# Layer 1's first 32-slot expert placed between the two fixed experts in the order of use

## The chip, the cores and the metric

The kernel runs on one core of a Trainium2 chip. The metric is the device time of one execution in microseconds (us), the median of three executions. Matrix products run on TensorE (PE), evictions and elementwise work on VectorE (DVE) and ScalarE (ACT), index work on GpSimd (POOL), and the transfers of weights from HBM to SBUF are issued by SyncE (SP).

## The reference

The model is a trunk of two layers over 256 latent tokens and 256 context tokens, D = 1024. Each layer mixes tokens and then applies a mixture of experts: a shared router picks two of 16 experts for each token, and an expert is a gated feed-forward with 512 hidden columns. In the last layer only the 256 latent tokens are used, so 512 assignments are spread over 16 experts.

```python
u = jax.nn.silu(xb @ w1[e]) * (xb @ w3[e])      # 1024 -> 512, twice
return (u @ w2[e]) * wt[:, None]                # 512 -> 1024, weighted
...
return jnp.zeros_like(h).at[buf_tok].add(y)     # summed back into the tokens
```

After layer 1's experts a residual sum and a final RMSNorm give the output. Everything is float32.

## The kernel before

The change concerns the experts of layer 1, the last part of the program, in `moe(1)`, whose matmuls run from about 1195 us to 1437 us of the trace.

**Experts and slots.** The experts have fixed numbers of token slots. Experts 0 and 1 are "fixed" (`s0`, `s1`): 96 slots each, handled as 64 + 32. The other 14 are ranked on the chip by how many tokens chose them and go by their rank, 0 to 13: ranks 0 and 1 have 96 slots, 2 to 5 have 64, 6 to 13 have 32 (`DCAP`). Which expert's weights a rank needs is known only after the router, so their loads read an expert number into a register first (L1631), and the address is computed from it. The weights of s0 and s1 have known addresses.

**Steps.** An expert is 12 chunks of weights of 128x1024 (512 KB): 8 "up" chunks (w1 and w3 for 128 rows of D) and 4 "down" chunks (w2). `steps_of(l)` turns the order of use into steps: the 8 up steps of an expert, then the 4 down steps of the expert before it in the order. One step is one chunk: `up()` (L1487) multiplies it with the gathered tokens `xs` and sums in PSUM; `down()` (L1550) multiplies it with the transposed hidden values `uf`. A chunk of a 64 + 32 expert takes two matmuls of 64 rows x 512 columns and four of 32 rows x 256 columns; a chunk of a 32-slot expert takes the four alone. The small matmuls use 64-column or 32-column parts of the array, placed by `tile_position`.

**What follows an up block.** With the last up chunk ACT takes silu (L1497) and DVE the product (L1498); both read the PSUM tile `mm`, of which layer 1 has two. Then `turn()` transposes u on PE (L1518), four steps later as a rule. The down results go to `ys`, and once a unit of 128 slots is complete, `combine` scales it and PE adds it into the tokens' accumulators (L1449).

**Gathered tokens.** `batch()` gathers the tokens of several experts at once by one-hot matmuls (L1386) and turns the one-hot table for the combine (L1372). The third batch holds ranks 6 to 13. A batch is started up to `LEAD` = 14 steps ahead of the first step that needs it, one piece a step.

**Weights and buffers.** `fetch()` issues the load of each step's chunk on SP in the order of the steps (L1634), as far ahead as a buffer is free. There are 25 buffers: 16 `eraw`, in use since the token mixing, and 9 `eraw2`. `expert_raw()` takes them by a running number i: of each 25, the first 16 from the one pool and the next 9 from the other. The 24 chunks of s0 and s1 are loaded before the router ends: 16 into `eraw`, 6 into `eraw2` (L1024), two into a spare part of another tile (`xT`). Three `eraw2` are left for the first loads of a ranked expert; every later load waits until PE has used the chunk whose buffer it takes. 168 such loads follow (14 experts of 12 chunks). SP never has more than eight of them outstanding, each with a semaphore of its own.

**Order.** The order of use of layer 1 is a table, `ORDER1` (L80). PE's instructions stand in the order of the steps, with transposes, gathers and combines put between them.

Of the kernel before, what the change touches and what calls it, by code (L numbers as in the profile page):

```python
# [76 lines left out]
NRAW = (13, 16)  # L77
LENT = (tuple(("y", i) for i in (16, 17, 18)), ())
ORDER0 = ("s0", "s1", 13, 0, 12, 1, 11, 2, 9, 3, 4, 8, 5, 6, 7, 10)
ORDER1 = ("s0", "s1", 13, 12, 11, 10, 0, 9, 1, 8, 2, 3, 7, 4, 5, 6)  # L80
ORDER = (ORDER0, ORDER1)
LEAD = 14
OVERFLOW0 = (6, 11)
# [1849 lines left out]
```

## Time and profile before

| | |
|---|---|
| time before, median of 3 (lowest to highest) | 1469.04 us (1467.43 to 1472.51) |
| the profiled execution's own time | 1461.18 us |
| its span in the trace | 1459.1 us |
| PE busy over the span | 1336.4 us (92%) |
| first matmul of an expert of layer 1 to last | about 1195.8 to 1437.4 us |
| HBM read over the span | 344.39 MB, 246 GB/s |

The trace is of one execution; its own time is what the terms of a sum are added to. Shares over the span mix the token mixing, where PE is the limit, with the experts, where the weights must be streamed, so the stretch from 1195 us on is read by itself.

### The profile page before, as it was taken

How to read it: one execution, taken by the hardware profiler on the slowest of the kernel's cores; microseconds unless marked ns; L12 is line 12 of the kernel's file. 1: busy time of each engine (PE TensorE's matmuls, PEld its weight loads, DVE VectorE, ACT ScalarE, POOL GpSimd, SP SyncE). 2: the span in 40 equal slices, each digit the busy share in tenths (PEclk: the TensorE clock that was granted, in tenths of full speed). 3: DMA queues.
4: the chain of work that ended last, by engine and by line, in shares of the span. 5: the costliest groups of instructions: out<-in, count | busy, mean ns of one | idle time of the engine just before them, and what ended most of it. 6: DMA issues, size and time to landing. Idle time of an engine off the chain costs nothing. (4 is left out here: it accounts for less than half of the span.)

```text
span 1459.1 us, 22788 instructions
## 1 busy us (share of the span) xinstructions
PE 1336.4 (92%) x8584; PEld 919.1 (63%) x8584; DVE 782.9 (54%) x1488; ACT 525.6 (36%) x834; POOL 134.5 (9%) x163
## 2 busy tenths in 40 slices
PE   4899999999999998999899669999999979999875
PEld 2677677777788675655556257778799843534323
DVE  2896775464545365555566248877655572322113
ACT  2523543432223223445555234255354431212102
POOL 0000000131211021012000030001022000000000
PEclk9999999999999999999999879999999979999996
DMA  9777222233362279999999585753259547999993
GB/s 353 256 279 278 66 91 90 88 130 130 130 210 100 81 275 328 358 410 410 410 410 385 185 332 184 277 178 117 91 182 355 192 156 251 369 408 409 408 409 129
DMA packets 99682, 361.14 MB, mean 247 GB/s; under 512 B 11504, under 2 KB 13680, under 8 KB 99312
## 3 DMA queue, kind: packets, MB, share of 16 engines
q1 hardware_dynamic: 91376, 331.97, 61.2%
q0 software_dynamic: 8192, 27.66, 5.0%
q8 instruction: 69, 1.13, 0.3%
q14 instruction: 45, 0.37, 0.1%
HBM read 344.39 MB, written 15.20 MB: 246 GB/s over the span
## 5 line engine op out<-in xcount | busy, mean ns | idle before, releaser
L527 PE MATMUL mm<-hH,whi 128*128 128x512 f32 (+1 forms) x928 | 323.8, 350 | 4.3 <-ACT k L947 2.2
L528 PE MATMUL mm<-hL,whi 128*128 128x512 f32 (+1 forms) x928 | 318.6, 344 | 1.5 <-DVE hL L409 1.5
L529 PE MATMUL mm<-hH,wlo 128*128 128x512 f32 (+1 forms) x928 | 318.6, 344 | 0.1
L216 DVE TENSOR_TENSOR wlo<-raw,whi 128x1280 fp32r<-128x1280 f32 (+1 forms) x124 | 186.2, 1503 | 66.4 <-ACT whi L215 65.5
L215 ACT ACTIVATE whi<-raw 128x1280 fp32r<-128x1280 f32 (+1 forms) x124 | 144.9, 1169 | 167.1 <-PE mm L528 99.3
L527 PEld LDWEIGHTS mm<-hH,whi 128*128 128x128 f32 x928 | 177.1, 191 | 41.1 <-issue 16.7
L529 PEld LDWEIGHTS mm<-hH,wlo 128*128 128x128 f32 x928 | 177.0, 191 | 27.8 <-issue 7.9
L528 PEld LDWEIGHTS mm<-hL,whi 128*128 128x128 f32 x928 | 177.3, 191 | 22.0 <-issue 2.3
L1487 PE MATMUL mm<-eraw,xs 128*32 128x256 f32 (+1 forms) x1376 | 164.7, 455 | 13.5 <-DMA eraw<-wexp_d 6.8
L216 DVE TENSOR_TENSOR wlo<-eraw,whi 128x1024 fp32r<-128x1024 f32 x96 | 115.6, 1223 | 29.9 <-ACT whi L215 24.8
L1487 PEld LDWEIGHTS mm<-eraw,xs 128*32 128x32 f32 (+1 forms) x1376 | 50.3, 119 | 108.5 <-issue 70.3
L215 ACT ACTIVATE whi<-eraw 128x1024 fp32r<-128x1024 f32 x96 | 99.4, 1056 | 32.1 <-PE mm L1480 20.2
L947 ACT ACTIVATE k<-mm,hbg 128x512 f32<-128x512 f32 (+1 forms) x64 | 37.2, 581 | 161.5 <-PE mm L529 161.5
L1498 DVE TENSOR_TENSOR u<-u,mm 64x256 f32<-64x256 f32 (+1 forms) x27 | 14.0, 531 | 136.5 <-ACT u L1497 136.3
L953 POOL TENSOR_TENSOR acc<-acc,k 128x512 f32<-128x512 f32 (+1 forms) x48 | 50.6, 1054 | 320.8 <-DVE k L952 320.8
L952 DVE SCALAR_TENSOR_TENSOR k<-k,mm 128x512 f32<-128x512 f32 (+1 forms) x48 | 26.6, 554 | 93.8 <-PE mm L529 93.8
L1550 PE MATMUL mm<-eraw,uf 128*32 128x256 f32 (+1 forms) x560 | 65.3, 442 | 3.6 <-DVE u L1498 1.7
L1497 ACT ACTIVATE u<-mm 64x256 f32<-64x256 f32 (+1 forms) x27 | 12.5, 465 | 154.0 <-PE mm L1487 154.0
L1479 PE MATMUL mm<-wlo,xh 128*128 128x512 f32 x128 | 51.7, 404 | 1.7 <-DVE wlo L216 1.6
L1480 PE MATMUL mm<-whi,xl 128*128 128x512 f32 x128 | 50.2, 392 | 0.0
L1478 PE MATMUL mm<-whi,xh 128*128 128x512 f32 x128 | 46.2, 412 | 3.3 <-ACT whi L215 3.3
L818 ACT ACTIVATE k<-aux,sm 128x512 f32<-128x512 f32 (+1 forms) x48 | 29.2, 613 | 47.8 <-DVE sm L816 43.9
(388 smaller groups left out, 1964.4 us busy)
## 6 DMA issues: line engine op xcount, KB each, us to landing
eraw<-wexp_d SPq DMA_DIRECT2D x379, 512.0 KB, 10.1
raw<-wgb_d SPq DMA_DIRECT2D x64, 640.0 KB, 3.9
mb<-wmod_d SPq DMA_DIRECT2D x48, 512.0 KB, 5.4
raw<-win_d SPq DMA_DIRECT2D x40, 512.0 KB, 6.5
mraw<-wmod_d SPq DMA_DIRECT2D x16, 512.0 KB, 5.2
raw<-wo_d SPq DMA_DIRECT2D x16, 512.0 KB, 3.5
eraw<-wmod_d SPq DMA_DIRECT2D x12, 512.0 KB, 5.4
ybuf<-k POOLq DMA_DIRECT2D x9, 512.0 KB, 3.3
```

Of the source, the lines that this page charges most:

```text
L215: S.activation(hi, src, AF.Copy)
L216: V.tensor_sub(lo, src, hi.bitcast(F32))
L527: PE.matmul(ps[:, :T_], lhsT=hi[:, ws], rhs=xh(xs), start=(i == 0), stop=False)
L528: PE.matmul(ps[:, :T_], lhsT=hi[:, ws], rhs=xl(xs), start=False, stop=False)
L529: PE.matmul(ps[:, :T_], lhsT=lo[:, ws], rhs=xh(xs), start=False, stop=(i == N - 1))
L947: S.activation(t, ps[:, :T], AF.Tanh, scale=0.5, bias=hbg[:, br * 8 + m:br * 8 + m + 1])
L953: ga = G.tensor_add(acc[:, m], acc[:, m], pr)
L1478: PE.matmul(ps, lhsT=xh[:, k], rhs=hi[:, o:o + 512], start=(k == 0), stop=False)
L1479: PE.matmul(ps, lhsT=xh[:, k], rhs=lo[:, o:o + 512], start=False, stop=False)
L1480: PE.matmul(ps, lhsT=xl[:, k], rhs=hi[:, o:o + 512], start=False, stop=(k == KT - 1))
L1487: PE.matmul(ps[n * g:n * g + n, :w], lhsT=xin[x, s0][0][:, k], rhs=r[:, g * w:(g + 1) * w], start=(k == 0), stop=(k == KT - 1), tile_posit ...
L1550: PE.matmul(e["pys", s0][n * g:n * g + n, :w], lhsT=e["uf", s0][:, k], rhs=r[:, g * w:(g + 1) * w], start=(k == 0), stop=(k == 3), tile_po ...
```

## The change

One line: in layer 1's order, rank 13 (32 slots) stands between s0 and s1. From 11 on the order is as before.

```diff
-ORDER1 = ("s0", "s1", 13, 12, 11, 10, 0, 9, 1, 8, 2, 3, 7, 4, 5, 6)
+ORDER1 = ("s0", 13, "s1", 12, 11, 10, 0, 9, 1, 8, 2, 3, 7, 4, 5, 6)
```

Blocks on PE before: s0 up, s1 up, s0 down, 13 up, s1 down, 12 up, 13 down, 11 up, 12 down, ... After: s0 up, 13 up, s0 down, s1 up, 13 down, 12 up, s1 down, 11 up, 12 down, ... The third batch, in which 13 is, is needed at step 8 instead of step 16, so its gather moves ahead, into s0's up block. `fixed_of(1)` follows the order too: the 16 chunks that go into `eraw` are s0's up and down and the first four of s1's up; `eraw2` takes the last four of s1's up and two of its down chunks (before: s0's four down and two of s1's).

PE, behind the last up chunk of s0 (`eraw_9962`), before: 16 gather matmuls of the third batch, then s1's first up chunk (`eraw_10007`).

```order
L1487 MATMUL mm_10845<-eraw_9962,xs_10785 64x512 x2
L1487 MATMUL mm_10846<-eraw_9962,xs_10785 32x256 x4
L1386 MATMUL aux_10917<-oh_10891,hTH_10554 128x256
L1386 MATMUL aux_10917<-oh_10891,hTL_10556 128x256
...
L1386 MATMUL aux_10936<-oh_10891,hTL_10557 128x256
L1487 MATMUL mm_10928<-eraw_10007,xs_10786 64x512 x2
L1487 MATMUL mm_10929<-eraw_10007,xs_10786 32x256 x4
```

The same place after: 13's up chunks follow at once, and s0's transposes (`u_10982`, `u_10985`) stand behind the second of them.

```order
L1487 MATMUL mm_10845<-eraw_9962,xs_10785 64x512 x2
L1487 MATMUL mm_10846<-eraw_9962,xs_10785 32x256 x4
L1487 MATMUL mm_10990<-eraw2_10959,xs_10874 32x256 x4
L1487 MATMUL mm_10990<-eraw2_10974,xs_10874 32x256 x4
L1518 MATMUL aux_11001<-cst_65,u_10982 128x64 x4
L1518 MATMUL aux_11008<-cst_65,u_10985 128x64 x2
L1487 MATMUL mm_10990<-eraw2_10988,xs_10874 32x256 x4
```

The gather has gone ahead of this place, and 13's accumulator `mm_10990` opens directly behind the matmuls of s0.

PE, from s1's last up chunk (`eraw2_10543`) to its first down chunk (`eraw2_10545`), after. `uf_11090` is 13's hidden values, `mm_11221` is 12's up block.

```order
L1487 MATMUL mm_11093<-eraw2_10543,xs_10786 32x256 x4
L1550 MATMUL mm_11170<-eraw_11146,uf_11090 32x256 x4
...
L1550 MATMUL mm_11170<-eraw_11175,uf_11090 32x256 x4
L1518 MATMUL aux_11207<-cst_65,u_11162 128x64 x4
L1518 MATMUL aux_11214<-cst_65,u_11165 128x64 x2
L1487 MATMUL mm_11221<-eraw_11190,xs_10874 32x256 x4
...
L1487 MATMUL mm_11221<-eraw2_11250,xs_10874 32x256 x4
L1550 MATMUL aux_11267<-eraw2_10545,uf_11212 64x512 x2
```

Before, s1's down chunks came directly behind 13's up block:

```order
L1487 MATMUL mm_11109<-eraw_11148,xs_10916 32x256 x4
L1487 MATMUL mm_11109<-eraw_11154,xs_10916 32x256 x4
L1550 MATMUL aux_11171<-eraw2_10545,uf_11100 64x512 x2
L1550 MATMUL aux_11172<-eraw2_10545,uf_11105 32x256 x4
L1550 MATMUL aux_11171<-eraw2_10547,uf_11100 64x512 x2
```

So 13's four down chunks and 12's eight up chunks have moved ahead of s1's down chunks.

SP, after, the 20th to the 28th load of a ranked expert (`wexp_d`), with what each waits for: `DMAHW` is the semaphore of an earlier transfer, `PE` a matmul that used the buffer before.

```order
L1634 DMA eraw2_11250<-wexp_d 128x1024 [waits DMAHW2_49]
...
L1634 DMA eraw2_11298<-wexp_d 128x1024 [waits DMAHW4_49]
...
L1634 DMA eraw2_11324<-wexp_d 128x1024 [waits DMAHW5_49,PE_49]
...
L1634 DMA eraw2_11359<-wexp_d 128x1024 [waits DMAHW0_49,PE_49]
...
L1634 DMA eraw2_11365<-wexp_d 128x1024 [waits DMAHW2_49,DMAHW1_49,PE_49]
...
L1634 DMA eraw2_11371<-wexp_d 128x1024 [waits PE_49]
```

The 23rd to the 26th (`eraw2_11324` to `eraw2_11359`) take the buffers of s1's last four up chunks, the 27th (`eraw2_11365`) waits for 12's last up chunk and the 28th (`eraw2_11371`) for s1's first down chunk. Before, the 28th waited for s1's second down chunk.

## Rows read from the trace of the kernel before

**Rows 1.** The page's head.

```profile
span 1459.1 us, 22788 instructions
```

**Rows 2.** Busy time by stretch: window, length, engines busy (instructions), PE's granted clock, DMA.

```profile
core 0: us, PE busy (x) PEld busy (x) DVE busy (x) ACT busy (x) POOL busy (x), PEclk, DMA share, GB/s
1195.00:1250.00 55.00, 54.99 (x422) 19.75 (x420) 18.19 (x57) 9.86 (x23) 1.42 (x6) 1.00 0.76 256
1250.00:1260.00 10.00, 9.99 (x132) 5.64 (x132) 3.67 (x7) 3.25 (x7) 0.00 (x0) 1.00 1.01 399
1250.00:1400.00 150.00, 138.16 (x1230) 58.36 (x1226) 34.91 (x77) 28.47 (x64) 0.00 (x0) 0.98 1.03 408
1410.00:1420.00 10.00, 6.76 (x52) 1.57 (x48) 1.80 (x3) 0.59 (x1) 0.00 (x0) 1.00 1.03 410
1420.00:1430.00 10.00, 8.39 (x44) 2.29 (x46) 0.71 (x2) 0.38 (x1) 0.00 (x0) 0.50 1.02 408
```

**Rows 3.** SP's waits in 1195 to 1250: us in total, times, longest.

```profile
SPq L1634 <- PE mm L1487: 23.5, 13, 4.3
SPq L1634 <- PE aux L1550: 10.3, 6, 5.2
```

**Rows 4.** SP's waits in 1250 to 1425, the largest.

```profile
SPq L1634 <- DMA eraw<-wexp_d: 90.8, 128, 1.8
```

**Rows 5.** SP's timeline: start, length; loads 1, 28, 44 and 168 of 168.

```profile
1192.96 0.35 SPq L1634 DMA_DIRECT2D eraw<-wexp_d  x1
...
1248.03 0.33 SPq L1634 DMA_DIRECT2D eraw<-wexp_d  x1
...
1263.66 0.33 SPq L1634 DMA_DIRECT2D eraw<-wexp_d  x1
...
1423.98 0.33 SPq L1634 DMA_DIRECT2D eraw<-wexp_d  x1
```

**Rows 6.** Line 1634, issue to landing: the first 28 loads.

```profile
L1634 SPq DMA_DIRECT2D eraw<-wexp_d x28: 332/333/347, 1193.0 to 1248.0; - x28
...
DMA to landing us min/median/max: 3.3/4.5/5.4
```

**Rows 7.** The same for all 168 loads.

```profile
DMA to landing us min/median/max: 3.3/10.1/11.2
```

**Rows 8.** PE's timeline in 1204 to 1252: start, length; two records to a matmul of L1487 and L1550.

```profile
1204.04 7.96 PE L1487 MATMUL mm<-eraw,xs 128*64 128x512 f32 x58
1211.92 0.39 PE L1386 MATMUL aux<-oh,hTH 128*128 128x256 f32 x1
...
1217.70 1.07 PE L1487 MATMUL mm<-eraw,xs 128*64 128x512 f32 x2
1218.70 0.39 PE L1386 MATMUL aux<-oh,hTH 128*128 128x256 f32 x1
...
1226.45 4.80 PE L1487 MATMUL mm<-eraw,xs 128*64 128x512 f32 x36
1231.19 6.38 PE L1550 MATMUL aux<-eraw,uf 128*64 128x512 f32 x48
1237.39 1.03 PE L1487 MATMUL mm<-eraw,xs 128*32 128x256 f32 x10
1238.42 0.46 PE L1518 MATMUL aux<-cst,u 64*128 64x64 f32 x4
...
1242.89 1.93 PE L1487 MATMUL mm<-eraw,xs 128*32 128x256 f32 x30
1244.74 3.23 PE L1550 MATMUL aux<-eraw,uf 128*64 128x512 f32 x24
```

**Rows 9.** DVE's timeline, the products of s0.

```profile
1212.10 1.03 DVE L1498 TENSOR_TENSOR u<-u,mm 64x512 f32<-64x512 f32 x2 [9.39 <-ACT u L1497]
```

**Rows 10.** PE's timeline in 1326 to 1329; in brackets the idle time before and its releaser.

```profile
1327.63 1.07 PE L1550 MATMUL mm<-eraw,uf 128*32 128x256 f32 x16 [0.84 <-DVE u L1498]
```

**Rows 11.** PE's timeline near the end.

```profile
1408.25 1.08 PE L1487 MATMUL mm<-eraw,xs 128*64 128x512 f32 x4 [0.20 <-DMA eraw<-wexp_d]
...
1435.93 1.50 PE L1550 MATMUL mm<-eraw,uf 128*32 128x256 f32 x24
```

## The prediction

> **What bounds the kernel now.** I read the busy time by stretch first. From 1250 to 1400 us the weights stream at 408 GB/s with a DMA share of 1.03, and in 1410 to 1420 PE works only 6.76 of 10 us while the stream goes on at 410 [rows 2]: there the transfers are the bound. From 1195 to 1250 it is the reverse: PE is busy 54.99 of 55.00 us, and the transfers run at 256 GB/s with a share of 0.76 [rows 2]. SP's waits say why. In 1195 to 1250 it waited for PE's up chunks (23.5 us in 13 waits) and down chunks (10.3 us in 6) [rows 3]; those are buffers not yet free. Behind 1250 it waited for earlier transfers, 90.8 us in 128 waits [rows 4], which is a full queue. So the experts of layer 1 have an opening, paced by how fast PE frees buffers, and a long stream behind it, paced by HBM.
>
> The turn from the one to the other is load 28 of 168: it left at 1248.03 [rows 5], when PE was through with s1's second down chunk, whose buffer it takes. From load 44 (1263.66) to load 168 (1423.98) are 124 intervals in 160.3 us, 1.29 each [rows 5], steady to the end. PE close to the end waits 0.20 us before each chunk for its landing [rows 11], so it follows the loads. A shift of load 28 therefore arrives at the end of the kernel, unless the stream makes it up; and with a share of 1.03 it has nothing to make it up with. The question is when load 28 goes in the changed order.
>
> **The work ahead of load 28.** In the changed order it waits for s1's first down chunk, not the second. Ahead of that stand, as before, s0's up and down, 13's up, s1's up and the third batch's gather; new are 13's four down chunks and 12's eight up chunks, and one down chunk of s1 is no longer ahead.
>
> - A chunk of a 32-slot expert: 1242.89 to 1244.74 are 30 records, 15 matmuls, 3.75 chunks, so 0.49 us each [rows 8]. Twelve of them are 5.9 us.
> - A chunk of a 64 + 32 expert: four down chunks from 1231.19 to 1237.39 are 1.55 each, three up chunks from 1226.45 to 1231.19 are 1.58 [rows 8]. One fewer is -1.6.
> - 13's two transposes of u come ahead too: four of 1518 took 0.46 [rows 8], so some 0.3 for two with their change of shape.
>
> These give +4.6 us.
>
> **What the interleaving costs.** Where other work cuts into a chunk, matmuls that ran side by side stand alone. The lone 64-row matmul at 1217.70 kept PE until 1218.70, 1.00 us [rows 8]. A whole chunk with two of these and four small ones is 1.58, of which the four small ones are 0.49, so the two side by side take 1.09: the lone one costs as much as the pair. Likewise the row at 1237.39 is one chunk and one lone 32-row matmul in 1.03 us [rows 8], so the lone one costs 0.54, as much as four. The changed order cuts two pairs of big matmuls (by the gather in s0's sixth chunk, by the combine in s1's second) and three sets of four (in s0's fifth and s1's first and second chunks). Extra: 2 x 1.00 for pairs and 3 x 0.5 for sets, 3.5 us. Before, one pair was cut, and 13's up block several times, of which only the place at 1237.39 lost one such 0.5, since elsewhere the pieces of neighbouring chunks joined to fours (15 in 1.85 us at 1242.89 [rows 8]); 1.5 us in front of load 28. Net +2.0. Should cutting turn out free, this term is 0; were each cut to cost a small chunk more, it would be 3.
>
> The Trainium skill has a rule that speaks against such cuts: "TensorEngine Tiling (Array Packing)", Key Properties, says that changing the tiling mode, not merely the tile, drains TensorE. By it each cut is paid in full, as the term above has it; without it the sum below would be 5.8 instead of 7.8. The trace agrees as far as it goes, with the lone matmul's 1.00 us.
>
> **Two new waits on PE.** Layer 1 has two `mm` accumulators, and an up block of 64 + 32 holds both until DVE has made the products.
>
> - Behind s0's up, PE went on at 1211.92 with 16 gather matmuls [rows 8], and DVE's two products ran from 1212.10 to 1213.13 [rows 9]; the first was through near 1212.6. Now 13's up stands there with a new accumulator and must wait for it: 0.7 us. Queued behind are 13's other up chunks and s0's transposes; the loads of 12's up wait for the former. The bounds: 0, if the evictions come earlier; 1.2, if it is both products.
> - Behind s1's up, 13's first down chunk opens an `mm` tile in the same way. The nearest row is the same pattern further on, 0.84 us behind an up block [rows 10]. Before, s0's down chunks stood there, in `aux` tiles; I take 0.8.
>
> Together +1.5 (0 to 2.0).
>
> **What hides.** The gather moves, but its 32 matmuls stand ahead of load 28 in both. The fixed chunks are all in place before s0 begins. 13's first three up loads need no buffer; loads 4 to 8 wait for s0's first five up chunks, so load 8 leaves near 1208 and lands at most 5.4 later [rows 6], by 1213.7, while s0's up, with the gather and two cuts in it, ends near 1218.6 (1211.92 + 32 gather matmuls and the added cuts and unit turns). If that cover went, the price would be the landing's delay, at most 5.4. SP's register loads for several ranks now stand bunched, between loads 11 and 12 above all; SP idles there for buffers, so they cost nothing.
>
> Loads 20 to 22 find free buffers and go early, but SP issues in order and load 23 waits for s1's fifth up chunk. So the few early loads buy nothing: 28 is held by PE's progress, not by bandwidth. A little comes back: in 1250 to 1260 the stream ran at 399 rather than 409 GB/s [rows 2], since a few loads still met buffers in use, and behind the later load 28 PE is further on. That is 10 x (1 - 399/409), -0.3 us.
>
> **Sum.** 4.6 + 2.0 + 1.5 - 0.3 = +7.8 us: load 28 at about 1255.8, the last load at about 1431.8, the end 7.8 later. The profiled execution's own time is 1461.18 us with a span of 1459.1 [rows 1]; it would become 1469.0. The median of the runs, 1469.04, is 7.9 above that execution, and goes to 1476.8. I forecast 1477.
>
> **Rivals.**
>
> No change, within 0.3% (4.4 us, about what a measurement of this kernel can tell). Cuts and waits cost nothing, because PE would have been held there anyway, and only 4.6 - 0.3 = 4.3 us remain: 1473.3. Or some of the shift hides at the end: the last load left at 1423.98 and, by the median of 10.1 [rows 7], landed at 1434.1, while PE came to the last four chunks at 1435.93 [rows 11]; 1.8 us of a late landing cost nothing if PE's work there does not move as well. 7.8 - 1.8 = 6.0 is by itself still slower; with one of the two other terms smaller it is same. For it speaks that both terms come from single rows; against it that PE in 1195 to 1250 had no gap to hide them in. Chance 0.19.
>
> Faster. 13's short chunks free eight buffers 0.49 us apart, where s1's free them 1.58 apart. If these went to loads 23 to 28, the queue would be full from load 22 on, near 1230, and load 28 would leave six intervals later, 1230 + 6 x 1.29 = 1237.7, 10.3 us earlier than before: 1458.7. It decides at load 23: it is faster if that load finds a buffer that 13 or s0 has freed. Against it: by the order of instructions it waits for PE's use of one of s1's last four up chunks. Chance 0.05.
>
> Slower still, by the clock. In 1420 to 1430 the granted clock was 0.50, the lower level of 1.2 GHz, after a stretch in which PE was busy 6.76 of 10 us [rows 2]; in the opening it was 1.00, with PE never idle. The change puts two waits into the opening and, since PE is then further ahead of the stream, more waits for landings behind it. Were the clock to fall for 10 us in the opening, work of 5 us at full speed would come 5 us later: 1482. For it speaks that waits of this kind become more; against it that two of 0.8 us are far fewer than those of 1410 to 1420. Chance 0.12.
>
> The Trainium skill, "TensorE: Matmul & The Clock Gate", Part 1, describes the throttled clock as the default state which activity lifts; by it a pause in the opening can cost more than its length. Rows 2 agree that the low level followed a sparse stretch; nothing here shows it after waits as short as these.
>
> That the change does not do what it says can be left out: the instructions stand in the new order on PE and SP.
>
> **Chances.** Forecast and its neighbourhood (slower, 1474 to 1481) 0.64, the clock 0.12, no change 0.19, faster 0.05. So slower 0.76, same 0.19, faster 0.05. The low end of the range is the 1473.3 of the second case less about 2.3 for the spread of the runs of before; the high end is the clock's 1482.
>
> **What would show it.** Load 28 issued near 1256 instead of 1248; a low stream (well under 400 GB/s) from about 1230 to 1255; PE waits of 0.7 to 0.8 us on DVE's product in front of 13's first up and first down chunks; the full stream from about 1256 to 1438; the last load near 1432. If load 23 leaves before s1's fifth up chunk is used, or the stream is full by 1240, my account of the buffers is wrong. If load 28 leaves near 1252, the cuts and waits cost nothing; if it leaves as expected and the end does not move, the stream was not the bound.

## The result, and the profile after

The changed kernel takes 1478.84 us, the median of six executions (1475.15 to 1482.68); the kernel before took 1468.21 over six (1464.24 to 1472.51). The ratio is 1.0069, with a 95% interval of 1.0053 to 1.0085: slower by some 10 us, where 7.8 were forecast.

The profiled execution took 1478.99 us. Its span is 18.2 us longer than that of before:

```profile
span 1477.3 us, 22773 instructions
```

Not all of that is the change. SP's timeline after shows the first load of a ranked expert (1), the 22nd, 23rd, 28th, 44th and the last of 168; start and length in us:

```profile
1200.37 0.35 SPq L1634 DMA_DIRECT2D eraw<-wexp_d  x1
...
1240.20 0.33 SPq L1634 DMA_DIRECT2D eraw<-wexp_d  x1
...
1252.70 0.33 SPq L1634 DMA_DIRECT2D eraw<-wexp_d  x1
...
1265.90 0.33 SPq L1634 DMA_DIRECT2D eraw<-wexp_d  x1
...
1281.46 0.33 SPq L1634 DMA_DIRECT2D eraw<-wexp_d  x1
...
1441.77 0.33 SPq L1634 DMA_DIRECT2D eraw<-wexp_d  x1
```

The first load left 7.4 us later than in the trace of before [rows 5]. The change did not do that: up to there every engine has the same instructions in the same order in both programs, and the only difference is which chunks of s0 and s1 are loaded first. The first of those loads (L310) left 6.8 us later already, before and after:

```profile
1100.74 0.43 SPq L310 DMA_DIRECT2D eraw<-wexp_d  x1
...
1107.50 0.42 SPq L310 DMA_DIRECT2D eraw<-wexp_d  x1
```

From the first load of a ranked expert on, load 28 left 65.5 us behind it, before 55.1: 10.5 later. From load 28 to the last are 175.9 us, before 175.95: nothing was made up and nothing lost. From the last load to the span's end are 35.5 us, before 35.1. So 7.4 + 10.5 - 0.1 + 0.4 = 18.2, and the change is worth the 10.5 at load 28.

The stretches say the same (columns as in rows 2). Here the opening has a DMA share of 0.63, the 10 us before load 28 only 0.54; behind it the stream is full.

```profile
1200.00:1255.00 55.00, 52.92 (x370) 20.95 (x368) 18.93 (x62) 10.01 (x23) 1.42 (x6) 0.95 0.63 217
1255.00:1265.00 10.00, 9.15 (x128) 4.07 (x126) 2.86 (x7) 2.09 (x5) 0.00 (x0) 1.00 0.54 175
1270.00:1400.00 130.00, 119.11 (x1036) 48.93 (x1036) 29.93 (x66) 23.95 (x55) 0.00 (x0) 0.97 1.03 408
```

SP's waits in 1200 to 1258 (us in total, times, longest) name the cause: up to 11.9 us at once for an up chunk on PE, which is load 23 behind load 22.

```profile
SPq L1634 <- PE mm L1487: 29.9, 14, 11.9
```

PE's timeline shows the price in front of load 28: the two new waits (in brackets: idle time and its releaser), 13's down chunks and 12's up block ahead of s1's down.

```profile
1224.22 1.65 PE L1487 MATMUL mm<-eraw,xs 128*64 128x512 f32 x12
1227.95 1.07 PE L1487 MATMUL mm<-eraw,xs 128*32 128x256 f32 x16 [2.08 <-DVE u L1498]
1228.95 0.90 PE L1518 MATMUL aux<-cst,u 64*128 64x64 f32 x6
1229.78 4.03 PE L1487 MATMUL mm<-eraw,xs 128*32 128x256 f32 x48
1233.74 6.38 PE L1550 MATMUL aux<-eraw,uf 128*64 128x512 f32 x48
...
1258.22 1.93 PE L1550 MATMUL mm<-eraw,uf 128*32 128x256 f32 x32 [0.84 <-DVE u L1498]
1260.09 0.58 PE L1518 MATMUL aux<-cst,u 64*128 64x64 f32 x6
1260.60 3.66 PE L1487 MATMUL mm<-eraw,xs 128*32 128x256 f32 x64
1264.19 2.23 PE L1550 MATMUL aux<-eraw,uf 128*64 128x512 f32 x14
```

The first wait is 2.08 us and not 0.7. DVE's timeline tells why: ACT was through with s0's silu near 1226.3, but DVE was still at work on the one-hot table of the next batch (L1357 to L1362, ranks 0 and 1), and the product stood behind it.

```profile
1226.10 0.29 DVE L1362 TENSOR_SCALAR oh<-ow 128x256 fp32r<-128x256 f32 x1
1226.31 0.41 DVE L1357 TENSOR_SCALAR oht<-sl,slf,w 128x256 f32<-128x256 f32 x1
1226.75 0.42 DVE L1361 TENSOR_TENSOR ow<-ow,oht 128x256 f32<-128x256 f32 x1
1227.21 1.03 DVE L1498 TENSOR_TENSOR u<-u,mm 64x512 f32<-64x512 f32 x2
```

PE had been busy without a gap up to that wait and was so again behind it. About 1 us behind the wait's end the granted clock fell to its lower level of 1.2 GHz and stayed there for some 3.4 us (1228.9 to 1232.3); the columns again as in rows 2:

```profile
1229.00:1232.00 3.00, 3.00 (x34) 1.74 (x34) 0.62 (x2) 0.00 (x0) 0.00 (x0) 0.50 0.06 25
```

Six chunks of 13 took 3.96 us there (1229.78 to 1233.74), 0.66 each instead of 0.49.

### The profile page after: what moved, and what is told of

It is laid out like the page before. It is cut to its first block, busy times and chain, and to the rows that moved or that the text cites. A ratio compares the mean times of both kernels' runs of the same rounds, so it can differ in the third digit from the quotient of the medians.

```text
span 1477.3 us, 22773 instructions
## 1 busy us (share of the span) xinstructions
PE 1348.9 (91%) x8584; PEld 924.7 (63%) x8584; DVE 783.2 (53%) x1488; ACT 525.3 (36%) x834; POOL 134.3 (9%) x163
## 5 line engine op out<-in xcount | busy, mean ns | idle before, releaser
L1487 PE MATMUL mm<-eraw,xs 128*32 128x256 f32 (+1 forms) x1376 | 169.1, 459 | 17.3 <-DMA eraw<-wexp_d 8.3
L1487 PEld LDWEIGHTS mm<-eraw,xs 128*32 128x32 f32 (+1 forms) x1376 | 51.2, 120 | 113.9 <-issue 71.8
L1498 DVE TENSOR_TENSOR u<-u,mm 64x256 f32<-64x256 f32 (+1 forms) x27 | 14.0, 531 | 140.3 <-ACT u L1497 140.3
L1550 PE MATMUL mm<-eraw,uf 128*32 128x256 f32 (+1 forms) x560 | 65.2, 442 | 4.6 <-DVE u L1498 2.5
L1497 ACT ACTIVATE u<-mm 64x256 f32<-64x256 f32 (+1 forms) x27 | 12.5, 464 | 153.5 <-PE mm L1487 153.5
```

Of the source, the lines that this page charges most:

```text
L1487: PE.matmul(ps[n * g:n * g + n, :w], lhsT=xin[x, s0][0][:, k], rhs=r[:, g * w:(g + 1) * w], start=(k == 0), stop=(k == KT - 1), tile_posit ...
L1550: PE.matmul(e["pys", s0][n * g:n * g + n, :w], lhsT=e["uf", s0][:, k], rhs=r[:, g * w:(g + 1) * w], start=(k == 0), stop=(k == 3), tile_po ...
```

## The experiments

The question was whether the time is lost because the stream of loads starts later (theory), or because PE itself does more and waits more (rival). The first four kernels set the one against the other. For each, the row of its load issues gives the first and the last of 168 starts; before it was 231.0 us from one to the other, after 241.4.

**a_release: the changed order, buffers taken as they come free.** Each load takes its buffer from the pool of the chunk that, in the order of the steps, PE leaves next. The rule for the pool becomes

```diff
-        if 0 <= i % (NRAW[l] + NRAW2[l]) - PRE[l] < NRAW2[l]:
+        if second_pool(l, i):
...
+def second_pool(l, i):
...
+    held = [c for c in fixed_of(l) if c not in lent] + [c for c in steps_of(l) if not isinstance(c[0], str)]
+    used = [held.index(c) for c in steps_of(l) if c not in lent]
+    return i - n < len(used) and second_pool(l, used[i - n])
```

> The changed order, but from the 25th buffer on a load takes whichever of the 25 buffers PE has left first, from either pool, instead of 16 of the one and then 9 of the other. PE's work and waits in the opening are those of the changed kernel. Theory of the entry to the stream (the change cost time because load 28 and all behind it left 10.5 us later): loads 23 to 31 now need s0's last down and s1's up chunks instead of waiting for 12's up block; the last load leaves about 229 us behind the first (changed kernel 241.4, before 231.0) and the time falls by about 12.6 us to 1466. Rival, the loss is PE's own (cuts, waits, slow clock: 6.4 us, and moved work): PE does the same, so the time stays within 0.3% of the changed kernel's 1478.8.

```profile
L1634 SPq DMA_DIRECT2D eraw<-wexp_d x168: 332/333/657, 1197.2 to 1427.7; - x168
```

230.5 us from first to last: 10.9 of the 241.4 - 231.0 and a little more came back, 1.5 short of the expectation. PE's waits in the opening are those of the changed kernel (waited for, us in total, times, longest):

```profile
PE mm L1487 <- DVE u L1498: 2.1, 1, 2.1
PE mm L1550 <- DVE u L1498: 0.8, 1, 0.8
```

The time is 1472.15 (12 runs), a ratio to before of 1.0015 (0.9998 to 1.0031), apart from the changed kernel's 1.0053 to 1.0085. It was to be 1466: the stream accounts for 10.9 us, the medians show 6.7. The profiled execution, whose first load left early (1197.2), was the fastest of the twelve at 1464.93; later starts of the others (on the scatter of the start, see below) would explain the rest, but no trace shows them. PE's cuts, waits and slow clock are all still in it, and most of the loss is gone: the rival falls.

**b_release: the order of before with the same rule for the buffers.** The same edit; PE's matmuls stand in the same order as before.

> The order of before, with the same rule for the buffers (first left, first taken). PE's instructions stand word for word as before. Theory of the entry: load 27 waits for 13's fourth up chunk, not for s1's first down chunk, so load 28 leaves some 7 us earlier behind the first load (48 instead of 55.1), the later ones a little less, and the time falls by about 4 us, to 1464. Rival, PE bound: no change, 1468 within 0.3%.

```profile
L1634 SPq DMA_DIRECT2D eraw<-wexp_d x168: 332/333/575, 1200.2 to 1428.5; - x168
```

228.3 us, 2.8 less than before, where 4 were expected; load 28 left 50.6 us behind the first instead of the 48 expected. The time is 1467.21, ratio 0.9988 (0.9973 to 1.0004): in the direction of the theory, but no more than the measurement can tell from no change.

**b_late: the order of before, with load 29 held up.** One load more from the second pool:

```diff
...
+    if l == 1 and i >= 41:
+        return i < 51 or (i - 51) % 25 >= 16
...
```

> The order of before, but one load more is taken from the second pool: load 29 must wait for 13's last down chunk, about 11 us later than it left before, and all behind it follow; later rounds of the two pools are moved by one. PE's order in the opening is that of before, nothing is cut and no wait on PSUM is added. Theory of the entry: the stream starts as late as in the changed kernel, the last load leaves about 241 to 242 us behind the first (231.0), and the time rises by 10 to 11 us to about 1479, as much as the change. Rival, PE's cuts and waits cost the time: none is here, so 1468 within 0.3%.

SP's timeline, load 1 and load 29, and the row of all loads:

```profile
1198.50 0.35 SPq L1634 DMA_DIRECT2D eraw<-wexp_d  x1
...
1265.22 0.33 SPq L1634 DMA_DIRECT2D eraw<-wexp_d  x1
```

```profile
L1634 SPq DMA_DIRECT2D eraw<-wexp_d x168: 332/333/801, 1198.5 to 1440.0; - x168
```

Load 29 left 66.7 us behind the first (before 55.6), and the last 241.5 behind it. The time is 1478.63, ratio 1.0061 (1.0044 to 1.0079): the loss of the change, made without the change, by a buffer alone.

**a_hold: the changed kernel, the one-hot table behind s0's products on DVE.**

```diff
...
+                    for ins in products.get("s0", ()) if last and b == 1 else ():
+                        held.enter_context(tc.issue_after(ins))
...
```

> The changed kernel, with the one-hot table of the batch of ranks 0 and 1 on DVE held back behind s0's two products. In the changed kernel PE waited 2.08 us for the first product in front of 13's up block, since four of the table's instructions stood ahead of it on DVE, and the clock was granted at 0.50 for some 3.7 us behind that wait. Theory: the wait becomes about 0.7 us as forecast, the clock stays at 1.00, load 28 leaves 2.7 us earlier behind the first load (62.8 instead of 65.5), and the time falls by about 2.7 us to 1476. If the clock falls all the same, only 1.4 us. Rival, the slow clock comes at some fixed place and not from the wait: the wait shrinks and the clock still falls.

PE's timeline at 13's up block (L1491 is L1487 of the other kernels, L1502 is L1498), and the clock behind it:

```profile
1230.09 1.07 PE L1491 MATMUL mm<-eraw,xs 128*32 128x256 f32 x16 [0.84 <-DVE u L1502]
1231.09 0.58 PE L1523 MATMUL aux<-cst,u 64*128 64x64 f32 x6
1231.61 2.80 PE L1491 MATMUL mm<-eraw,xs 128*32 128x256 f32 x48
1234.33 6.38 PE L1555 MATMUL aux<-eraw,uf 128*64 128x512 f32 x48
```

```profile
1231.00:1234.00 3.00, 3.00 (x54) 1.90 (x54) 2.87 (x10) 0.00 (x0) 0.34 (x1) 1.00 0.32 124
```

```profile
L1639 SPq DMA_DIRECT2D eraw<-wexp_d x168: 332/333/1317, 1203.5 to 1442.4; - x168
```

The wait is 0.84 us, the clock stays at 1.00, the same 48 records of 13's chunks take 2.72 us (1231.61 to 1234.33) instead of 3.96, and the stream is 238.9 us, 2.5 shorter, where 2.7 were expected. So wait and slow clock go together. The time does not show it: 1479.51 (6 runs), ratio 1.0067 (1.0051 to 1.0083), where 1476 was expected. In its trace the first load left at 1203.5, 3.1 us later than in the changed kernel's.

**b_again and a_again: both kernels once more.**

> The kernel before once more, for a second trace of it. The first trace had its first load of a ranked expert at 1192.96 us, the changed kernel's had it at 1200.37, though nothing ahead of that place is changed. If the 7.4 us are chance of the one execution (theory), this trace has it near 1200, as the other traces so far (1197 to 1203), while the last load leaves 231.0 us behind the first, within 0.5. Rival, the change delays the work ahead of the experts: the first load is again near 1193.

> The changed kernel once more. Theory: the last load leaves 241.4 us behind the first within 0.5, whatever the time at which the first one goes; the 2.08 us wait in front of 13's up block and the clock of 0.50 behind it come again.

The rows of the two, in this order:

```profile
L1634 SPq DMA_DIRECT2D eraw<-wexp_d x168: 332/333/635, 1201.4 to 1432.5; - x168
```

```profile
L1634 SPq DMA_DIRECT2D eraw<-wexp_d x168: 332/333/1017, 1202.8 to 1444.3; - x168
```

First to last is 231.1 and 241.5 us: the stretch that the change touches repeats within 0.1 us. What differs between executions of one program is the work ahead: the first load of before left at 1193.0 in one trace and at 1201.4 in the other. In a_again the 2.08 us wait stands again in front of 13's up block:

```profile
1230.64 1.07 PE L1487 MATMUL mm<-eraw,xs 128*32 128x256 f32 x16 [2.08 <-DVE u L1498]
```

The times: before against itself 1.0009 (0.9993 to 1.0025), the changed kernel 1483.03, ratio 1.0108 (1.0083 to 1.0133), which is 14 us and more than the 10.5 of the experts. Over the ten traces the first load left between 1193.0 and 1204.9: 1193.0 to 1201.4 in the four with the order of before, 1197.2 to 1204.9 in the six with a changed order. The orders have no part in it that these traces show: from the first load of a chunk of s0 in layer 1 (L310), ahead of which the programs do not differ, to the first load of a ranked expert the ten traces have 92.15 to 92.90 us, and both orders have values at either end (before 92.22, b_again 92.86; a_release 92.15, a_again 92.90). The scatter arises ahead of that place; what causes it is not known, and for the executions that were not profiled nothing is shown.

**a_release_hold: both edits on the changed order.**

> The changed order with both edits: buffers taken in the order in which PE leaves them, and the one-hot table held behind s0's products. Theory of the entry to the stream: the two gains add, the last load leaves 230.5 - 2.5 = 228.0 us behind the first, and the time is 3 us below the kernel before. Rival, the gains don't add, since with the buffers freed loads 23 to 28 no longer wait for what the hold brings forward: 230.5 and the time of before.

```profile
L1639 SPq DMA_DIRECT2D eraw<-wexp_d x168: 332/333/1100, 1204.7 to 1432.6; - x168
```

227.9 us: the gains add, to a stream 3.2 us shorter than before. The time is 1469.13, ratio 0.9999 (0.9985 to 1.0013): the 3 us do not show in the time. The first load of its trace left late again, at 1204.7; whether that is the whole reason is not shown.

**c_release_hold: both edits, and 13 and 12 ahead of s1.**

```diff
+ORDER1 = ("s0", 13, 12, "s1", 11, 10, 0, 9, 1, 8, 2, 3, 7, 4, 5, 6)
```

> Both edits, and ranks 13 and 12 placed ahead of s1, so that s1's up block, whose chunks are long, comes when short chunks have freed 24 buffers. Theory: load 28 leaves 41 to 45 us behind the first (before 55.1), the last about 225, and the time falls to about 1464, 6 us below before. Rival: PE must now wait for 12's weights in the opening and loses what the stream gains: last load 228 or more behind the first, time as before.

```profile
L1639 SPq DMA_DIRECT2D eraw<-wexp_d x168: 332/333/946, 1204.9 to 1430.3; - x168
```

225.4 us, as expected; load 28 left 44.5 us behind the first, and in the opening PE waited for no weights at all, as in the kernel before. The time is 1464.18 (12 runs), ratio 0.9968 (0.9948 to 0.9988): faster than both kernels, by 5 us against before, where 6 were expected.

## Why the prediction was right

**The bound.** Right. The end follows load 28: the 140 intervals behind it took 175.9 us in both kernels. b_late (the late load without PE's part) shows the whole loss, a_release (PE's part without the late load) hardly any.

**The work moved ahead.** Forecast +4.6. Measured: 13's down chunks 1.87, the transposes behind them 0.51, 12's up 3.59, less s1's chunk of 1.58, +4.4.

**The cuts.** Forecast 3.5 us gross, net +2.0. Pieces of s0's fifth and sixth chunks took 4.7 us against 3.2 uncut, those of s1's first and second 5.2 against 3.2: 3.6 gross, net +2.1. Here are the pieces of s1's first two chunks:

```profile
1240.05 1.63 PE L1487 MATMUL mm<-eraw,xs 128*64 128x512 f32 x6
1241.61 0.33 PE L1518 MATMUL aux<-cst,u 64*128 64x64 f32 x2
1241.88 1.64 PE L1487 MATMUL mm<-eraw,xs 128*32 128x256 f32 x8
1243.44 0.50 PE L1449 MATMUL acc<-ohs,yh 96*128 96x256 f32 x2
1243.87 1.62 PE L1487 MATMUL mm<-eraw,xs 128*64 128x512 f32 x4
1245.42 0.39 PE L1449 MATMUL acc<-ohs,yl 96*128 96x256 f32 x1
```

The three pieces take 1.56, 1.56 and 1.55 us to the row behind, and some 0.55 more go to the last three small matmuls later. This is read from PE's timeline: the rows show what a cut costs and not why, and no kernel without the cuts was run.

**The waits.** Behind s1's up 0.84 us, forecast 0.8. Behind s0's up 2.08, forecast 0.7, with a bound of 1.2: this term was too small. The step that took it from before's evictions overlooked that the gather, moved to an earlier place, lets the next batch's table onto DVE earlier as well, just ahead of the product. a_hold moves the table away and has 0.84.

**The clock.** It was kept as a rival of its own, of 5 us for 10 at half speed. It came in small: some 3.4 us at 0.50 behind the 2.08 us wait, which cost 1.2 us more for 13's chunks and 0.3 for the transposes. Each of the three traces with that wait has it, at 1.5 to 1.6 us, and it stands behind none of the waits of 0.84 us in the openings. So the forecast left out 1.5 us by taking the rival for all or nothing.

**The run-in.** Forecast -0.3, measured -0.1.

Together 4.4 + 2.1 + 2.9 + 1.5 - 0.1 = 10.8 us at the last load, where 10.4 were measured (241.4 against 231.0) and 7.8 forecast: waits and clock are the difference, and 0.4 us stay unexplained. The measured 1478.84 lies only 1.8 us from the forecast of 1477, and 0.8 us of that closeness is luck: the median of before fell from 1469.04 over three executions to 1468.21 over six.

**The rival "faster".** It stayed off exactly at its point: load 23 waited 12.5 us behind load 22 for s1's fifth up chunk. a_release gave loads 23 to 27 other buffers, and load 28 left 13 us earlier behind the first; yet the end only came back to that of before and did not go 10 below, since the later ones (28 to 31) then wait for s1's long chunks one by one, 1.58 us apart. That rival counted the buffers to load 28 only.

## What to carry to other kernels

Where a prefetch queue turns from waiting for buffers to a full stream, find the load at that turn, and list what the consumer must do before its buffer comes free: a change of order is worth what it adds to or takes from that list, and the fixed rule by which buffers go round can cost more than the order (10.9 us here). Long and short consumers side by side want buffers handed on in the order in which they come free. When a step moves to an earlier place, look also at what follows it on the other engines' queues, since it moves up too.

## What the runs showed of the hardware

A wait of 2.08 us on TensorE was followed by a granted clock of 0.50 for some 3.4 us, in the middle of a busy opening, in all three traces that have it; in the three with a wait of 0.84 us at the same place the clock stayed at 1.00. No length in between was run. From load 44 to the last the ten traces have 160.2 to 160.9 us for 124 intervals, so once full the stream kept its 1.29 us per 512 KB through every order tried. And the same program reached the same place at 1193.0 us in one execution and 1201.4 in another, with 0.1 us between the two in the stretch behind it: for a change of this size the interval between two rows of one trace tells more than the total.
